# Split-ahead weight units moved from SyncE's DMA queue to GpSimd's, with four smaller edits of order

## The chip, the cores and the metric

One NeuronCore of one Trainium2 chip runs the whole program. The metric is device time in microseconds (us) of that core, from the first to the last instruction and what lies around them. The engines named below are PE (TensorE), DVE (VectorE), ACT (ScalarE), POOL (GpSimd) and SP (SyncE, which only issues DMAs here). Each engine runs its own instructions strictly in the program's order; a DMA queue's transfers are issued by the engine that owns it, in that engine's order.

## The reference

Two layers on a sequence of 512 rows of width 1024, all in f32. A layer is a SwiGLU feed-forward block (FFN), a mixer, and a second FFN:

```
for i in range(2):
    x = x + 0.5 * swiglu_ffn(x, ffn1_norm[i], gate[i], up[i], down[i])
    h = rmsnorm(x, mix_norm[i])
    x = x + (even_mixer(h, ...) if i == 0 else odd_mixer(h, ...))
    x = x + 0.5 * swiglu_ffn(x, ffn2_norm[i], ...)
return rmsnorm(x, final_norm)
# swiglu_ffn: h = rmsnorm(x, g); (silu(h @ w_gate) * (h @ w_up)) @ w_down, with d_ff = 2816
# even_mixer: gMLP and an attention with compressed, selected and window branches, then @ w_out
# odd_mixer: two sparse attentions, then @ w_out
```

## The kernel before

Every large product is made of three matmuls in a rounded f32 format: a weight is cut into a high part `h` (an ACT copy, line 315) and the rest `l` (a DVE subtraction, line 316), an activation likewise, and `mm3` (lines 320 to 322) adds h*h, h*l and l*h. A weight unit is a tile of 128 x 1024 numbers, 512 KB.

**FFN weights** are loaded by SP (lines 296, 309, 683), cut by ACT and DVE and used at once; the pools `raw`, `wh` and `wl` have four buffers each. An FFN has 11 strips `k` of 256 columns in three groups (0 to 3, 4 to 7, 8 to 10). For a strip `gate_up` multiplies x by the gate weights, ACT applies Silu (line 765), GpSimd multiplies by the norm's factor (line 766), and `seven` makes the up product in seven quarter products, whose results ACT and DVE take out of PSUM (`k1`, line 726, and others). After a group, `proj_T` multiplies by the down weights.

**Mixer weights** are cut ahead of time. `cut_ahead` is a generator over 60 units (32 of the even mixer, 28 of the odd one): it loads a unit (`craw`, two buffers), cuts it into `ch` and `cl` (two buffers each), and stores both to DRAM (`cuth`, `cutl`). The mixers later load the two parts and cut nothing. The generator is stepped by `take` after some strips and by `weave` inside the down products. What finally decides the order on each engine is a scheduler, which moves these units earlier than the code has them wherever it thinks an engine free; so most units of the odd mixer too are cut during the first FFN.

**The first chunks of x** are transposed by PE into PSUM (line 871); `Norm.add` copies each of the eight to `x[c]` (DVE, line 522), and makes the high part `h` (ACT, line 523) and the low part `l` (DVE, line 524) that the first matmuls read.

**Norms.** `Norm.rstd` sums squares with PE (line 549) and takes a power on GpSimd (line 553); `rstd_row` spreads the result over a bank (line 561); `finish` ends strip 0, which waited for it. **load_early** loads the compressor's weights on ACT's DMA queue. In the even mixer `branches` rotates the queries (`rope`, line 251, on DVE) and then transposes them (line 871) after two `yield`s; `weave` puts filler matmuls between yields.

Of the kernel before, what the change touches and what calls it, by code (L numbers as in the profile page):

```python
# [13 lines left out]
F32 = mybir.dt.float32  # L14
F32R = mybir.dt.float32r
I32 = mybir.dt.int32
AF = mybir.ActivationFunctionType
# [48 lines left out]
def hybrid_kernel(tc, x_in, positions, ffn1_norm, ffn1_w_gate, ffn1_w_up, ffn1_w_down, mix_norm,  # L66
# [4 lines left out]
    with ExitStack() as ctx:  # L71
# [199 lines left out]
        def cut_ahead(units):  # L271

            raw = None
            for i, (key, src, a, b, rows) in enumerate(units):
                n = a * b
                if raw is None:
                    raw = load_raw(src, a, b, rows, "craw", 2)
                h, l = cut(raw, n, ("ch", "cl"), 2)
                if i + 1 < len(units):
                    raw = load_raw(*units[i + 1][1:], "craw", 2)  # L280
                parts = []
                for t, c in ((h, "h"), (l, "l")):
                    d = scr.tile([P, n], F32, tag=nm("cut" + c), name=nm("cut" + c))
                    nc.sync.dma_start(d, t[:, :n].bitcast(F32))
                    parts.append(d)
                cut_units[key] = parts
                yield

        def load_raw(src, a, b, rows, tag, bufs):
            n = a * b  # L290
            raw = sb.tile([P, 1024], F32, tag=tag, bufs=bufs, name=nm(tag))
            r3 = raw[:, :n].rearrange("p (a b) -> p a b", a=a)
            if rows:
                o = 0
                for sap in src:
                    pin(nc.sync.dma_start(r3[:, o:o + sap.shape[1]], sap))
                    o += sap.shape[1]
            elif isinstance(src, list):
                o = 0
                for sap, wd in src:  # L300
                    dst = r3[:, :, o:o + wd]
                    if len(sap.shape) == 4:
                        for c in range(a):
                            nc.sync.dma_start(dst[:, c].rearrange("p (k d) -> p k d", k=sap.shape[2]), sap[:, c])
                    else:
                        nc.sync.dma_start(dst, sap)
                    o += wd
            else:
                nc.sync.dma_start(r3, src)
            return raw  # L310
# [188 lines left out]
        class Norm:  # L499
# [17 lines left out]
            def add(self, c, src=None):  # L517

                g = gcol(self.which, self.layer, c)
                h, l = tile_("xg"), tile_("xg")  # L520
                if src is not None:
                    pin(nc.vector.tensor_copy(x[c], src))
                pin(nc.scalar.activation(h, x[c] if src is None else src, AF.Copy, scale=g))
                pin(nc.vector.scalar_tensor_tensor(l, x[c], g, h.bitcast(F32), op0=ALU.mult, op1=ALU.subtract))
                self.xg[c] = (h, l)
# [216 lines left out]
        def gate_up(wg, wu, k, norm, sums, at):  # L742
# [6 lines left out]
            for hf in range(2):  # L749
                h, l = wunit(wg[hf * 512:(hf + 1) * 512, f0:f0 + 256].rearrange("(c p) f -> p c f", p=P), 4, 256)  # L750
                if hf:
                    norm.finish()
                for f in range(2):
                    if f:
                        norm.rstd()
                    for c in range(4):
# [17 lines left out]
        def ffn(norm, wg, wu, wd, nxt, hook=None, ahead=iter(()), per=2, early=None):  # L774

            sums = Sums(norm)
            for p0, p1 in GROUPS:
                at = []
                for k in range(p0, p1):
                    gate_up(wg, wu, k, norm, sums, at)  # L780
                    if hook is not None and k < 6:
                        next(hook, None)
                    if k in (3, 5, 6, 7, 8, 9):
                        run(take(ahead, 1))
                for d0 in range(0, D, 256):
                    part = per / (4 * (p1 - p0)) if p1 < 11 or d0 < 512 else 0.0
                    run(weave(proj_T(wd[256 * p0:256 * p1], at, d0,
                                     lambda c, ps: update(c, ps, 0.5, nxt if p1 == 11 else None)), ahead, [part]))
                    if p1 == 11 and d0 == 512 and early is not None:
                        early()  # L790
# [302 lines left out]
        def even_mixer(norm, nxt, tab):  # L1093
# [174 lines left out]
            def branches(g):  # L1268
# [7 lines left out]
                rope(zq[NT], 0, NT, 4, tab)  # L1276
                yield
                yield
                qrot = []
# [312 lines left out]
```

## Time and profile before

| | us |
|---|---|
| median of 3 runs | 2017.83 (2011.75 to 2018.38) |
| profiled execution | 2025.39 |
| its span, first to last instruction | 2023.3 |
| PE busy in the span | 1964.5 (97%) |
| DVE, ACT, POOL busy | 1394.1, 889.1, 306.4 |

The profiled execution is one run, 7.6 us above the median. The share of busy time is a mean over stages: the first FFN (0 to about 400 us) keeps the DMA engines at 70 to 94% and PE has gaps there, while from 750 to 1400 us PE has next to none. "PEclk" is the clock that was granted to TensorE, 1.00 being 2.4 GHz; its other level is 1.2 GHz.

### The profile page before, as it was taken

What the parts mean: (1) busy time and instruction counts of PE and PEld (TensorE: products, weight loads), DVE (VectorE), ACT (ScalarE), POOL (GpSimd) and SP (SyncE); (2) the same over time, 40 slices, a digit from 0 to 9 for tenths busy, and PEclk for the clock granted to TensorE, in tenths of its full rate; (3) what the DMA queues carried; (4) which work ended last, traced back from release to release, by engine and by line L of the source; (5) the groups of instructions that cost most, each with busy time, mean ns of one, the idle gap of its engine ahead of it and who ended that gap; (6) DMA issues with size and microseconds to landing.
All of it is one profiled execution on the core that took longest, in us unless ns stands there. A gap on an engine that the chain in (4) does not pass through costs nothing.

```text
span 2023.3 us, 30245 instructions
## 1 busy us (share of the span) xinstructions
PE 1964.5 (97%) x11575; PEld 1738.2 (86%) x11575; DVE 1394.1 (69%) x2456; ACT 889.1 (44%) x1562; POOL 306.4 (15%) x370
## 2 busy tenths in 40 slices
PE   8999998999999999999999999999999999999998
PEld 6888888799987889898888889888999788889898
DVE  6877758655587587475667747566698788567464
ACT  5544434424567564243345424333336764334143
POOL 1201101012234211010101101010112202011012
PEclk9999999999999999999999999999999999999999
DMA  7698899988210223333232333323532232323321
GB/s 223 209 305 268 296 303 313 335 299 294 105 43 26 89 85 111 98 95 115 84 105 84 116 93 101 109 84 100 191 143 105 73 102 85 116 84 105 104 84 63
DMA packets 223873, 290.35 MB, mean 144 GB/s; under 512 B 26136, under 2 KB 191728, under 8 KB 223728
## 3 DMA queue, kind: packets, MB, share of 16 engines
q1 hardware_dynamic: 216800, 282.01, 42.9%
q10 hardware_dynamic: 6736, 6.37, 0.9%
q8 instruction: 91, 1.49, 0.3%
q14 instruction: 54, 0.44, 0.1%
q0 software_dynamic: 192, 0.04, 0.0%
HBM read 230.11 MB, written 58.26 MB: 143 GB/s over the span
## 4 chain that ended last, share of the span: by engine, by line
PE 62%; DVE 8%; ACT 2%; issue 1%; POOL 0%; ACTq 0%; POOLq 0%; DVEq 0%
PE psB L320 8%; PE psB L321 8%; PE psB L322 8%; PE psT L322 6%; PE psT L320 6%; PE psT L321 6%; PE psG L320 5%; PE psG L322 5%; PE psG L321 5%; PE psC L949 2%; DVE f L1417 1%; PE psT L939 1%; DVE sm L1416 1%; DVE p L916 1%; ACT p L918 1%
## 5 line engine op out<-in xcount | busy, mean ns | idle before, releaser
L316 DVE TENSOR_TENSOR wl<-raw,wh 128x1024 fp32r<-128x1024 f32 (+1 forms) x198 | 259.9, 1315 | 82.5 <-ACT wh L315 77.8
L315 ACT ACTIVATE wh<-raw 128x1024 fp32r<-128x1024 f32 (+1 forms) x198 | 197.4, 1003 | 219.9 <-PE psB L321 181.5
L766 POOL TENSOR_TENSOR p<-p,p 128x512 f32<-128x512 f32 x78 | 127.9, 1641 | 992.9 <-ACT p L765 954.3
L320 PE MATMUL psT<-xg,wh 128*128 128x512 f32 x704 | 275.6, 392 | 0.2 <-DVE k L734 0.2
L322 PE MATMUL psT<-xg,wl 128*128 128x512 f32 x704 | 274.8, 391 | 0.0
L321 PE MATMUL psT<-xg,wh 128*128 128x512 f32 x704 | 274.8, 390 | 0.0
L321 PE MATMUL psB<-f,wh 128*128 128x512 f32 x656 | 255.6, 390 | 1.8 <-DVE f L495 1.8
L320 PE MATMUL psB<-f,wh 128*128 128x512 f32 x656 | 255.6, 390 | 0.0
L322 PE MATMUL psB<-f,wl 128*128 128x512 f32 x656 | 255.2, 389 | 0.0
L320 PE MATMUL psG<-t7h,wh 128*128 128x256 f32 x624 | 180.3, 289 | 12.2 <-ACT k L726 9.5
L322 PE MATMUL psG<-t7h,wl 128*128 128x256 f32 x624 | 179.0, 287 | 3.6 <-DVE wl L694 3.6
L321 PE MATMUL psG<-t7l,wh 128*128 128x256 f32 x624 | 178.9, 287 | 0.0
L322 PEld LDWEIGHTS psT<-xg,wl 128*128 128x128 f32 x704 | 132.7, 189 | 27.9
L320 PEld LDWEIGHTS psT<-xg,wh 128*128 128x128 f32 x704 | 132.8, 189 | 27.0 <-DVE k L734 0.4
L321 PEld LDWEIGHTS psT<-xg,wh 128*128 128x128 f32 x704 | 132.6, 188 | 26.5
L320 PE MATMUL psB<-wh,xg 128*128 128x256 f32 x512 | 148.2, 289 | 2.3 <-DVE sa L916 1.3
L321 PEld LDWEIGHTS psB<-f,wh 128*128 128x128 f32 x656 | 123.2, 188 | 27.7 <-DVE f L495 2.6
L322 PE MATMUL psB<-wh,xg 128*128 128x256 f32 x512 | 145.4, 284 | 0.0
L321 PE MATMUL psB<-wl,xg 128*128 128x256 f32 x512 | 145.3, 284 | 0.0
L765 ACT ACTIVATE p<-p 128x512 f32<-128x512 f32 x78 | 49.2, 631 | 218.3 <-DVE p L764 218.1
L322 PEld LDWEIGHTS psB<-f,wl 128*128 128x128 f32 x656 | 123.2, 188 | 25.5
L320 PEld LDWEIGHTS psB<-f,wh 128*128 128x128 f32 x656 | 123.2, 188 | 25.3
(304 smaller groups left out, 4661.3 us busy)
## 6 DMA issues: line engine op xcount, KB each, us to landing
raw<-in_ffn_w_down_dram SPq DMA_DIRECT2D x168, 256.0 KB, 3.4
raw<-in_ffn_w_gate_dram SPq DMA_DIRECT2D x80, 512.0 KB, 3.8
raw<-in_ffn_w_up_dram SPq DMA_DIRECT2D x80, 512.0 KB, 4.0
cuth<-ch SPq DMA_DIRECT2D x44, 512.0 KB, 6.6
cutl<-cl SPq DMA_DIRECT2D x44, 512.0 KB, 6.7
wh<-cuth SPq DMA_DIRECT2D x44, 512.0 KB, 4.4
wl<-cutl SPq DMA_DIRECT2D x44, 512.0 KB, 4.0
craw<-in_od_w_in_dram SPq DMA_DIRECT2D x16, 512.0 KB, 6.6
```

Source lines behind the costliest of these rows:

```text
L315: pin(nc.scalar.activation(h[:, :n], raw[:, :n], AF.Copy))
L316: pin(nc.vector.tensor_sub(l[:, :n], raw[:, :n], h[:, :n].bitcast(F32)))
L320: nc.tensor.matmul(ps, lh, rh, start=start, stop=False)
L321: nc.tensor.matmul(ps, lh, rl, start=False, stop=False)
L322: nc.tensor.matmul(ps, ll, rh, start=False, stop=stop)
L765: nc.scalar.activation(g, g, AF.Silu)
L766: nc.gpsimd.tensor_mul(g, g, rb)
L916: nc.vector.tensor_tensor_reduce(out=pr[i], in0=bank[i], in1=bias(i), scale=-1.0, scalar=3e38, op0=ALU.add, op1=ALU.min, accum_out=ng[:, i ...
L918: nc.scalar.activation(pr[i], pr[i], AF.Exp, scale=-1.0, bias=ng[:, i:i + 1], accum_out=rs[:, i:i + 1])
L939: nc.tensor.transpose(ps[:, o:o + P], pr[i][:, j * P:(j + 1) * P], ident)
L949: nc.tensor.matmul(job["accs"][0][:, j * P:512], v(j), hl[j][part], start=first, stop=last)
L1416: nc.vector.max(out=m8, in_=bd[i])
```

## The change

Five edits:

1. `cut_ahead` issues its loads and its stores from GpSimd's queue, and stores a unit one step later, after the next unit's cut. 214 DMAs leave SP's queue and enter POOL's.
2. `Norm.add` makes `h` and `l` of the first chunks straight from PSUM; the copy to `x[c]` comes after them, on ACT.
3. `gate_up` of strip 1 calls `rstd` 12 matmuls later, and `finish` likewise.
4. The generator is no longer stepped after strips 8 and 9, and `load_early` runs after the first quarter of the last down product, not after the third.
5. `branches` yields YB = 5 times, not twice, between the rotation and the transposes.

```diff
         def cut_ahead(units):
-            raw = None
+            raw = done = None
+
+            def store():
+                key, n, tiles = done
+                parts = []
+                for t, c in zip(tiles, "hl"):
+                    d = scr.tile([P, n], F32, tag=nm("cut" + c), name=nm("cut" + c))
+                    nc.gpsimd.dma_start(d, t[:, :n].bitcast(F32))
+                    parts.append(d)
+                cut_units[key] = parts
+
             for i, (key, src, a, b, rows) in enumerate(units):
                 n = a * b
                 if raw is None:
-                    raw = load_raw(src, a, b, rows, "craw", 2)
-                h, l = cut(raw, n, ("ch", "cl"), 2)
+                    raw = load_raw(src, a, b, rows, "craw", 2, nc.gpsimd)
+                now = key, n, cut(raw, n, ("ch", "cl"), 2)
+                if done is not None:
+                    store()
+                done = now
                 if i + 1 < len(units):
-                    raw = load_raw(*units[i + 1][1:], "craw", 2)
-                parts = []
-                for t, c in ((h, "h"), (l, "l")):
-                    d = scr.tile([P, n], F32, tag=nm("cut" + c), name=nm("cut" + c))
-                    nc.sync.dma_start(d, t[:, :n].bitcast(F32))
-                    parts.append(d)
-                cut_units[key] = parts
+                    raw = load_raw(*units[i + 1][1:], "craw", 2, nc.gpsimd)
                 yield
-
-        def load_raw(src, a, b, rows, tag, bufs):
+            store()
+
+        def load_raw(src, a, b, rows, tag, bufs, queue=nc.sync):
...
                 h, l = tile_("xg"), tile_("xg")
+                v = x[c] if src is None else src
+                pin(nc.scalar.activation(h, v, AF.Copy, scale=g))
+                pin(nc.vector.scalar_tensor_tensor(l, v, g, h.bitcast(F32), op0=ALU.mult, op1=ALU.subtract))
                 if src is not None:
-                    pin(nc.vector.tensor_copy(x[c], src))
-                pin(nc.scalar.activation(h, x[c] if src is None else src, AF.Copy, scale=g))
-                pin(nc.vector.scalar_tensor_tensor(l, x[c], g, h.bitcast(F32), op0=ALU.mult, op1=ALU.subtract))
+                    pin(nc.scalar.copy(x[c], src))
...
                 if hf:
-                    norm.finish()
+                    norm.rstd()
                 for f in range(2):
-                    if f:
-                        norm.rstd()
+                    if hf and f:
+                        norm.finish()
...
-                    if k in (3, 5, 6, 7, 8, 9):
+                    if k in (3, 5, 6, 7):
                         run(take(ahead, 1))
...
-                    if p1 == 11 and d0 == 512 and early is not None:
+                    if p1 == 11 and d0 == 0 and early is not None:
                         early()
...
-                yield
-                yield
+                for _ in range(YB):
+                    yield
```

Where the change adds lines ahead of them, later lines have higher numbers after it: 766 is 777, 871 is 882, 315 is 325.

On POOL, between the products of strips 2 to 4 of the first FFN (p is the Silu result, tile p_1541 is strip 4's), there was nothing else before:

```order
L766 TENSOR_TENSOR p_673<-p_673,p_427 128x512
L766 TENSOR_TENSOR p_677<-p_677,p_427 128x512
L766 TENSOR_TENSOR p_886<-p_886,p_427 128x512
L766 TENSOR_TENSOR p_890<-p_890,p_427 128x512
L766 TENSOR_TENSOR p_1541<-p_1541,p_427 128x512
L766 TENSOR_TENSOR p_1545<-p_1545,p_427 128x512
```

The same place now, from two DMAs ahead of strip 3's products on (craw is a load, cuth and cutl are stores):

```order
L282 DMA cuth_1893<-ch_1460 128x1024
L316 DMA craw_1897<-in_ev_w_in_dram 128x4x256
L777 TENSOR_TENSOR p_886<-p_886,p_427 128x512
L777 TENSOR_TENSOR p_890<-p_890,p_427 128x512
L282 DMA cutl_1895<-cl_1461 128x1024
L282 DMA cutl_2113<-cl_1890 128x1024
L282 DMA cuth_2111<-ch_1889 128x1024
L316 DMA craw_2115<-in_ev_w_in_dram 128x4x256
```

50 DMAs now stand between strip 3's second product and strip 4's first, and 44 between strip 7's and strip 8's.

On ACT, at the start of the program, the first rows before were these (xg is a chunk's high part, wh the first FFN weights', p_153 a square):

```order
L523 ACTIVATE xg_112<-psX_107,keep 128x512
L315 ACTIVATE wh_120<-raw_117 128x512
L531 ACTIVATE p_153<-x_92 128x512
L523 ACTIVATE xg_131<-psX_126,keep 128x512
L315 ACTIVATE wh_139<-raw_136 128x512
L315 ACTIVATE wh_170<-raw_167 128x1024
```

and they are these now:

```order
L532 ACTIVATE xg_112<-psX_107,keep 128x512
L325 ACTIVATE ch_1068<-craw_1065 128x840
L535 COPY x_92<-psX_107 128x512
L325 ACTIVATE wh_120<-raw_117 128x512
L532 ACTIVATE xg_131<-psX_126,keep 128x512
L542 ACTIVATE p_153<-x_92 128x512
L325 ACTIVATE ch_1102<-craw_1072 128x840
L535 COPY x_93<-psX_126 128x512
L325 ACTIVATE wh_139<-raw_136 128x512
```

The first split-ahead cuts (ch) have moved ahead of the first FFN weights' cuts. The second of the two DMAs that fill craw_1065 waits for the first.

On PE, in the even mixer, the transposes of the rotated queries (z_4200) of the first head group stood seven filler matmuls into a weight strip, eight together:

```order
L322 MATMUL psB_4462<-wh_4543,xg_3575 128x256
L320 MATMUL psB_4462<-wh_4543,xg_3588 128x256
L871 MATMUL psX_4523<-keep,z_4200 128x128
L871 MATMUL psX_4523<-keep,z_4200 128x128 x3
L871 MATMUL psX_4550<-keep,z_4200 128x128 x4
L321 MATMUL psB_4462<-wl_4545,xg_3588 128x256
```

They now stand 24 matmuls into it, in two fours with nine matmuls between:

```order
L332 MATMUL psB_4462<-wh_4532,xg_3698 128x256
L882 MATMUL psX_4574<-keep,z_4200 128x128
L882 MATMUL psX_4574<-keep,z_4200 128x128 x3
L330 MATMUL psB_4463<-wh_4532,xg_3616 128x256
L331 MATMUL psB_4463<-wl_4534,xg_3616 128x256
L332 MATMUL psB_4463<-wh_4532,xg_3617 128x256
```

## Rows read from the trace of the kernel before

**Rows 1.** The page: engines' busy time; GpSimd's product by the norm's factor.

```profile
PE 1964.5 (97%) x11575; PEld 1738.2 (86%) x11575; DVE 1394.1 (69%) x2456; ACT 889.1 (44%) x1562; POOL 306.4 (15%) x370
...
L766 POOL TENSOR_TENSOR p<-p,p 128x512 f32<-128x512 f32 x78 | 127.9, 1641 | 992.9 <-ACT p L765 954.3
```

**Rows 2.** Windows of the first 500 us, by stage.

```profile
core 0: us, PE busy (x) PEld busy (x) DVE busy (x) ACT busy (x) POOL busy (x), PEclk, DMA share, GB/s
0.00:44.00 44.00, 36.75 (x153) 28.47 (x153) 31.43 (x48) 24.77 (x34) 2.98 (x23) 0.96 0.72 220
44.00:103.00 59.00, 54.93 (x284) 47.59 (x285) 48.37 (x68) 31.53 (x42) 16.27 (x14) 0.97 0.71 217
103.00:309.00 206.00, 198.91 (x1073) 172.54 (x1072) 146.20 (x206) 83.21 (x108) 14.51 (x9) 0.99 0.88 291
309.00:356.00 47.00, 41.29 (x238) 36.97 (x237) 40.85 (x53) 26.16 (x35) 7.70 (x5) 0.93 0.94 322
356.00:460.00 104.00, 99.11 (x630) 91.40 (x630) 61.82 (x133) 37.44 (x68) 14.80 (x24) 0.98 0.90 316
460.00:500.00 40.00, 37.02 (x297) 36.55 (x296) 20.55 (x40) 19.73 (x39) 6.58 (x10) 0.96 0.87 299
```

**Rows 3.** Waits of PE, whole span: us in total, times, longest us.

```profile
PE psG L320 <- ACT k L726: 9.5, 5, 5.3
PE psX L871 <- DVE z L251: 6.4, 5, 3.0
...
PE psS L321 <- DMA wl<-cutl: 2.6, 1, 2.6
```

**Rows 4.** Waits of ACT, whole span: the longest of those for split-ahead DMAs.

```profile
ACT ch L315 <- DMA craw<-in_ev_w_in_dram: 23.9, 8, 5.6
```

**Rows 5.** DMA issues: engine, count, KB each, median us to landing.

```profile
cuth<-ch SPq DMA_DIRECT2D x44, 512.0 KB, 6.6
...
craw<-in_ev_w_in_dram SPq DMA_DIRECT2D x4, 384.0 KB, 5.0
...
craw<-in_ev_w_in_dram SPq DMA_DIRECT2D x4, 36.0 KB, 2.4
```

**Rows 6.** Timeline of ACT at strips 3, 4, 8, 9: start, duration, [idle before].

```profile
102.62 0.61 ACT L765 ACTIVATE p<-p 128x512 f32<-128x512 f32 x1
...
166.15 0.63 ACT L765 ACTIVATE p<-p 128x512 f32<-128x512 f32 x1 [3.52 <-DVE p L764]
...
308.56 1.06 ACT L315 ACTIVATE ch<-craw 128x1024 fp32r<-128x1024 f32 x1 [6.45 <-DMA craw<-in_od_w_in_dram]
309.53 0.61 ACT L765 ACTIVATE p<-p 128x512 f32<-128x512 f32 x1
...
336.46 0.62 ACT L765 ACTIVATE p<-p 128x512 f32<-128x512 f32 x1
```

**Rows 7.** Timeline of POOL: its DMAs (16, 16 and 4 rows).

```profile
67.61 0.78 POOL L63 DMA_DIRECT2D rows<-in_mix_norm_dram  x1
...
69.89 0.48 POOL L63 DMA_DIRECT2D rows<-in_ev_cmp_pos_v_dram  x1
70.36 0.52 POOL L63 DMA_DIRECT2D pos_i<-in_positions_dram  x1
```

**Rows 8.** Timeline of the opening, ACT then PE.

```profile
6.66 0.62 ACT L315 ACTIVATE wh<-raw 128x512 fp32r<-128x512 f32 x1
...
23.49 0.90 ACT L315 ACTIVATE ch<-craw 128x840 fp32r<-128x840 f32 x1 [3.01 <-DMA craw<-in_ev_w_in_dram]
...
25.54 0.49 PE L320 MATMUL psS<-xg,wh 128*128 128x512 f32 x1 [1.80 <-ACT xg L523]
```

**Rows 9.** Timeline of PE, even mixer and norm of the second FFN.

```profile
484.21 0.28 PE L322 MATMUL psB<-wh,xg 128*128 128x256 f32 x1
484.33 0.28 PE L320 MATMUL psB<-wh,xg 128*128 128x256 f32 x1
487.59 1.94 PE L871 MATMUL psX<-keep,z 128*128 128x128 f32 x8 [2.98 <-DVE z L251]
...
721.85 1.19 PE L549 MATMUL psX<-keep,p 128*128 128x2 f32 x8 [1.96 <-DVE p L535]
```

More of the change, by code (lines that the diff above doesn't have):

```diff
@@ L295, in load_raw @@
                 for sap in src:
-                    pin(nc.sync.dma_start(r3[:, o:o + sap.shape[1]], sap))
+                    pin(queue.dma_start(r3[:, o:o + sap.shape[1]], sap))
                     o += sap.shape[1]
@@ L303, in load_raw @@
                         for c in range(a):
-                            nc.sync.dma_start(dst[:, c].rearrange("p (k d) -> p k d", k=sap.shape[2]), sap[:, c])
+                            queue.dma_start(dst[:, c].rearrange("p (k d) -> p k d", k=sap.shape[2]), sap[:, c])
                     else:
-                        nc.sync.dma_start(dst, sap)
+                        queue.dma_start(dst, sap)
                     o += wd
             else:
-                nc.sync.dma_start(r3, src)
+                queue.dma_start(r3, src)
             return raw
```

## The prediction

> **What bounds the kernel now.** I read the page first: PE is busy 97% of the span, no other engine over 69% [rows 1]. So a gain can only come out of PE's idle time and out of the time in which its clock is low. The windows say where that is [rows 2]. For each stage the reader is to see two losses: length minus PE busy, and (1 - PEclk) times length, since a stretch at 1.2 GHz does half the work. They give 7.2 + 1.8 us for 0 to 44, 4.1 + 1.8 for 44 to 103, 7.1 + 2.1 for 103 to 309, 5.7 + 3.3 for 309 to 356, 4.9 + 2.1 for 356 to 460, and 3.0 + 1.6 for 460 to 500. So 44 to 356 us, the first FFN's strips and down products, loses 24.1 us, and all 500 us lose 45.
>
> Then the waits of PE [rows 3]: the longest is for `k1`, an ACT copy in `seven`, up to 5.3 us at once. ACT's timeline says why [rows 6]: at 308.56 it starts a split-ahead cut after waiting 6.45 us for that unit's load, and strip 8's Silu and the `k1` copy stand behind it in ACT's order. One group of such waits alone holds ACT 23.9 us in all [rows 4]. In the same stages the DMA engines are busy 71 to 94% [rows 2]. So PE is stalled here by an in-order ACT that waits for split-ahead data.
>
> **The change, part by part.** The 0.3% by which a measurement of this kernel can tell a change from none is 6 us.
>
> *A, the opening.* Removed: eight DVE copies; ACT's wait of 3.01 us for the second unit, which stood between two chunks and gave PE a gap of 1.80 us [rows 8], after which the clock lost the stage's 1.8 us [rows 2]. The second unit's cut has moved ahead of the second weights' cut and the third comes after seven weight cuts, so this should go: -3.6. Added: the first unit's cut stands ahead of the first weights' cut on ACT, and its second load waits for its first to land. With the load issued at about 1 us and the medians 5.0 and 2.4 us [rows 5], the cut can start at 8.4; with 2.4 for each, at about 5.8, when the chunk's own high part is just done. The cut takes 0.90, the copy of x about 0.6, and the weights' cut, which began at 6.66 [rows 8], begins between 7.5 and 9.9: 0.9 to 3.2 late, with PE waiting. I take 1.6, nearer the low end, because the loads now go out first. A = -2.
>
> *B, strips and down products to strip 9.* The units are not only on another queue, the scheduler also places them earlier. Counted in ACT's order, the cuts that stand ahead of strip 3's second Silu are 13 (8 before), of strip 8's first 55 (40 before), of strip 9's second 60 (43 before). ACT can't pass a cut before its load has landed and the store two units back has left its buffer, so these bytes must have moved by then. Between strip 3 (102.62) and strip 8 (309.53) [rows 6] there are now 42 units, 57.1 MB of loads and stores, beside 36 FFN weight units of 0.524 MB, 18.9 MB: 76.0 MB. Before it was 32 units and 60.3 MB, and 291 GB/s for 206 us, 59.9 MB, is what the windows have [rows 2]. How fast can it go? The two fullest stages moved 322 GB/s at a share of 0.94 and 316 at 0.90 [rows 2], 343 and 351 at a full share; I take 347. About 3.5 MB are in flight ahead of need at the start, as before. (76.0 - 3.5) / 0.347 = 209 us, so strip 8's Silu comes at 311.6 in place of 309.5. From there to strip 9's second Silu 9.9 MB take 28.5 us: 340.1 against 336.46 [rows 6]. PE's own work between strips 3 and 8 would need 207 less the 9.2 us lost there, 198, so DMA decides: B = +3, with the 24.1 us of old losses already inside it. Ends: if the queues leave the share at 0.94 (322 GB/s), 225 and 31 us give 358.5, B = +22; if DMA never binds, all the losses go, B = -24.
>
> By the Trainium skill's page DMA: Bandwidth & Descriptors, section Issuing engines are not separate DMA queues, DMAs started by different engines run on the same 16 DMA engines and interleave, and a second issuer saves only the time to issue. By that rule the move itself gains nothing in B (rival 3 below); the trace agrees so far that the shares are those of a nearly full resource, and no run here shows two full queues.
>
> What the second queue can do is keep the share up. SP's loads of FFN weights no longer stand behind stores that wait for a cut, and the split-ahead chain no longer behind weight loads that wait for a buffer. That is why I take the full share.
>
> POOL pays for it. Its DMAs with 4 to 16 rows cost 0.48 to 0.78 us each [rows 7], as much with 4 as with 16. A DMA of 128 rows costs 0.5 us if it goes by the instruction, 6.2 us if by the row (0.78 x 8). Between strip 3's product and strip 4's, 50 DMAs have to go out in about 62 us, 1.24 us each. I take 0.8, since 4 and 16 rows cost the same, and 50 x 0.8 = 40 fits into 62. The products themselves (1.64 us, [rows 1]) are needed only after `seven`, so a few us of lateness cost nothing. If this cover is gone, it is rival 2.
>
> *C, 356 to 460 us.* Before, the last cuts stood in the down product of strips 8 to 10 and in the even mixer; now none does. The wait of 2.6 us for the mixer's first weight unit [rows 3] came while DMA was 90% busy, and the clock lost 2.1 us in that stage [rows 2]. About 4.7 of the 7.0 us lost there go. With `load_early` moved into the emptier place: C = -5. It is between 0 (the loads still come late) and -7.
>
> *D, YB.* PE waited 2.98 us for the rotation [rows 9]. 17 more filler matmuls, 0.12 us apart [rows 9], now stand ahead: 2.0 us of the wait filled, and a gap of 1.0 should leave the clock alone (1.6 us lost in that stage, [rows 2]). D = -3.5, between 0 and -4.6; the later jobs start that much later, which PE's other filler covers.
>
> *E, rstd and finish.* In the second FFN PE waited 1.96 us before the sums of squares [rows 9]. In the built order these matmuls keep their place among the strip's matmuls, only the transposes of `rstd_row` move by 12. So the wait stays: E = 0 (to -3.7 if it went).
>
> Sum: -2 + 3 - 5 - 3.5 = -7.5 us. Against the profiled execution's 2025.4 that is 2017.9; that run lay 7.6 above the median of the runs shown, 2017.8, so for runs like those I expect **2010 us**.
>
> **The rivals.**
>
> 1. *The bytes bind harder (slower).* The split chain has two buffers at each step, and each step waits for a landing; stores took 6.6 us to land [rows 5]. If the share stays at 0.94, B is +22 and the sum +11.5: 2029. It decides the sign from B = +10.5, that is from 337 GB/s on downward (82.4 MB in 244.4 us). For it: no stage so far was over 0.94. Against it: in all of them weights and split units shared one queue.
>
> 2. *POOL becomes the bound (slower).* 214 DMAs and 22 products have to go through it by strip 10. At 1.5 us for a DMA that is 357 us, where there are about 334: B = +23 and the time 2030; at 2 us it would be over 2100. It decides from about 1.3 us per DMA. For it: nothing in the trace shows a POOL DMA of 128 rows. Against it: 4 rows cost as much as 16.
>    The Trainium skill's page SBUF: State Buffer, section SBUF: two separate sides, speaks for this rival: GpSimd writes the descriptors of its DMAs itself, and a DVE operation in a two-port mode locks it out meanwhile. Its figures, 620 ns for a DMA alone and about 3100 beside a DVE copy, would make 133 or 663 us of the 214, no change of the sum or a loss of hundreds. No run here shows it; DVE's work in this stage is mostly two-input subtractions, not copies.
>
> 3. *The queue doesn't matter.* ACT waits for the same bytes at the same places, its lead eaten by the earlier cuts: B = 0, A = 0, C half. With D that is -6 at best, -3 if the filled wait turns up at the next transposes: 2012 to 2015, which I count as the same.
>
> 4. *DMA never binds (faster).* With its own queue the chain runs ahead of ACT, and PE's 24 us go: sum -34.5, 1983. For it: the present waits come from late issues as well as from full engines. Against it: 76 MB in the 198 us that PE needs are 384 GB/s, more than any stage had.
>
> **How the numbers follow.** Chances: my forecast (2003 to 2017) 0.37, rival 1 0.17, rival 2 0.12, rival 3 0.17, rival 4 and what lies between it and the forecast 0.17. The forecast's range reaches six parts in seven below 2011.8, the bound of faster; counting a part of it and rival 3 as the same: faster 0.48, same 0.24, slower 0.28. The range, 1988 to 2036, leaves out the lower half of rival 4 and the upper part of rivals 1 and 2, about 2 in 10.
>
> **What would show it.** A: PE's first product matmuls 1 to 3 us later than now, and no gap before the fifth chunk. B: strip 8's first Silu at 305 to 318 us, the DMA share above 0.94 between 103 and 336, and ACT's waits for split-ahead loads longer, not shorter; POOL's DMAs at 0.5 to 1 us. C: no wait of PE for the mixer's first unit. D: the wait before the rotated transposes at 1 us or less. E: the wait before the sums still near 2 us. I am wrong if POOL's products start many us after their Silu, if the share stays where it is, or if strip 8 comes before 300 us.

## The result: 2083.6 us, 3.3% slower

The changed kernel takes 2083.62 us (median of 4 runs, 2079.16 to 2087.26) where the kernel before takes 2016.91 (4 runs beside it): a ratio of 1.0334 [1.0305, 1.0364]. The forecast was 2010, the range ended at 2036. The profiled execution of the changed kernel took 2085.85 us, its span 2084.1; against the 2023.3 us of before, 60.8 us more.

The page of the changed kernel: busy time of the engines, and the two DMA queues (packets, MB, share of the 16 engines' time). [rows 1] has the same line of before.

```profile
PE 1979.7 (95%) x11575; PEld 1751.5 (84%) x11575; DVE 1389.0 (67%) x2448; ACT 893.2 (43%) x1570; POOL 430.2 (21%) x584
...
q1 hardware_dynamic: 161152, 197.75, 29.6%
q0 software_dynamic: 23776, 84.30, 11.6%
```

GpSimd's queue (q0) now carries 84.30 MB. POOL has 214 instructions more and is busy for 123.8 us more; one of these DMAs lasts 0.64 us on the mean (a store 0.55, a load 0.73 to 0.76). No engine but PE is near its limit.

Its windows, cut where the same strips begin and end as in [rows 2] (52, 111, 364 and 419 us answer to 44, 103, 309 and 356):

```profile
0.00:52.00 52.00, 37.55 (x164) 29.45 (x165) 33.82 (x47) 33.46 (x48) 20.37 (x48) 0.99 0.91 297
52.00:111.00 59.00, 53.64 (x274) 46.28 (x273) 47.54 (x65) 31.60 (x42) 31.16 (x43) 0.95 0.80 259
111.00:364.00 253.00, 210.67 (x1061) 182.01 (x1060) 160.95 (x214) 94.11 (x118) 101.44 (x151) 0.90 0.89 306
364.00:419.00 55.00, 45.90 (x245) 41.20 (x245) 40.55 (x53) 23.42 (x32) 19.33 (x24) 0.87 0.59 210
419.00:522.00 103.00, 101.99 (x674) 95.48 (x674) 51.15 (x126) 29.22 (x63) 12.14 (x23) 1.00 0.56 193
```

Read as the prediction read them: the third row loses 42.3 us to idle time of PE and 25.3 to its clock, where before lost 7.1 and 2.1. The DMA share there is 0.89, as before (0.88): the second queue has not filled the engines. After 419 us PE is better off than before (1.0 us idle in 103, clock 1.00).

ACT's timeline: the Silu of strip 3 (the second), 4 (first), 8 (first) and 9 (second); [rows 6] has them of before at 102.62, 166.15, 309.53 and 336.46.

```profile
110.74 0.63 ACT L776 ACTIVATE p<-p 128x512 f32<-128x512 f32 x1 [0.21 <-DVE p L775]
...
193.80 0.63 ACT L776 ACTIVATE p<-p 128x512 f32<-128x512 f32 x1 [2.17 <-DVE p L775]
...
364.41 0.63 ACT L776 ACTIVATE p<-p 128x512 f32<-128x512 f32 x1 [5.75 <-DVE p L775]
...
396.95 0.61 ACT L776 ACTIVATE p<-p 128x512 f32<-128x512 f32 x1
```

They are 8.1, 27.7, 54.9 and 60.5 us late. So the opening and strips 0 to 3 lost 8.1 us, the stretch from there to strip 9 52.4, and all that follows 0.3. Where the largest single step lies, between 160 and 191 us, ACT's timeline shows how (ch is a split-ahead cut; wh at L325 and L704 is an FFN weight's):

```profile
160.99 1.06 ACT L325 ACTIVATE ch<-craw 128x1024 fp32r<-128x1024 f32 x1 [4.53 <-DMA craw<-in_ev_w_out_dram]
161.95 1.04 ACT L325 ACTIVATE wh<-raw 128x1024 fp32r<-128x1024 f32 x1
170.71 0.63 ACT L325 ACTIVATE ch<-craw 128x512 fp32r<-128x512 f32 x1 [7.71 <-DMA craw<-in_ev_w_out_dram]
171.25 0.61 ACT L704 ACTIVATE wh<-raw 128x512 fp32r<-128x512 f32 x1
177.24 1.06 ACT L325 ACTIVATE ch<-craw 128x1024 fp32r<-128x1024 f32 x1 [5.38 <-DMA craw<-in_ev_w_out_dram]
178.20 1.04 ACT L704 ACTIVATE wh<-raw 128x1024 fp32r<-128x1024 f32 x1
181.22 0.63 ACT L325 ACTIVATE ch<-craw 128x512 fp32r<-128x512 f32 x1 [1.97 <-DMA cuth<-ch]
186.77 1.06 ACT L325 ACTIVATE ch<-craw 128x1024 fp32r<-128x1024 f32 x1 [4.92 <-DMA craw<-in_ev_w_out_dram]
187.73 1.04 ACT L704 ACTIVATE wh<-s 128x1024 fp32r<-128x1024 f32 x1
```

Each weight's cut stands right behind a split-ahead cut that waits 4.5 to 7.7 us for its load. DVE makes the low parts of the same weights (wl), and it waits for other data: for the landing of a split-ahead store that must leave its buffer, and for the up weights of the FFN, which it adds to sums (s).

```profile
179.51 1.22 DVE L326 TENSOR_TENSOR cl<-craw,ch 128x1024 fp32r<-128x1024 f32 x1 [5.73 <-DMA cutl<-cl]
...
181.25 1.21 DVE L705 TENSOR_TENSOR wl<-raw,wh 128x1024 fp32r<-128x1024 f32 x1
...
190.21 0.69 DVE L720 TENSOR_TENSOR s<-raw,raw 128x512 f32<-128x512 f32 x1 [7.14 <-DMA raw<-in_ffn_w_up_dram]
...
191.95 1.22 DVE L705 TENSOR_TENSOR wl<-s,wh 128x1024 fp32r<-128x1024 f32 x1
```

The waits of PE between 170 and 194 us (in total, times, longest):

```profile
PE psG L330 <- ACT wh L704: 6.4, 2, 3.8
PE psG L332 <- DVE wl L705: 6.3, 2, 3.6
```

PE waits 12.7 us for just these cuts, half of it for ACT's and half for DVE's, in gaps of 2.6 to 3.8 us, and the clock falls to its lower level for part of the time. The window has:

```profile
170.00:194.00 24.00, 11.25 (x51) 9.37 (x52) 9.24 (x12) 6.61 (x9) 9.43 (x16) 0.72 0.84 286
```

PE is busy for 11.25 of 24 us, at a mean clock of 0.72.

### The profile page after: what moved, and what is told of

It reads as the page before. It is cut to its first block, busy times and chain, and to the rows that moved or that the text cites. A ratio compares the mean times of both kernels' runs of the same rounds, so it can differ in the third digit from the quotient of the medians.

```text
span 2084.1 us, 30295 instructions
## 1 busy us (share of the span) xinstructions
PE 1979.7 (95%) x11575; PEld 1751.5 (84%) x11575; DVE 1389.0 (67%) x2448; ACT 893.2 (43%) x1570; POOL 430.2 (21%) x584
## 3 DMA queue, kind: packets, MB, share of 16 engines
q0 software_dynamic: 23776, 84.30, 11.6%
## 4 chain that ended last, share of the span: by engine, by line
PE 61%; issue 12%; DVE 12%; DMA 9%; POOL 3%; ACT 3%; DVEq 0%; POOLq 0%; ACTq 0%
PE psB L330 8%; PE psB L331 8%; PE psB L332 8%; PE psT L331 5%; PE psT L330 5%; PE psT L332 5%; PE psG L330 5%; PE psG L332 5%; PE psG L331 5%; DMA cutl<-cl 4%; DMA raw<-in_ffn_w_up_dram 2%; DMA craw<-in_ev_w_in_dram 2%; DVE cl L326 1%; ACT p L929 1%; DVE f L1428 1%
## 5 line engine op out<-in xcount | busy, mean ns | idle before, releaser
L777 POOL TENSOR_TENSOR p<-p,p 128x512 f32<-128x512 f32 x78 | 123.2, 1582 | 758.2 <-ACT p L776 730.4
L325 ACT ACTIVATE wh<-raw 128x1024 fp32r<-128x1024 f32 (+1 forms) x198 | 197.4, 1003 | 189.8 <-PE psB L331 162.1
L330 PE MATMUL psG<-t7h,wh 128*128 128x256 f32 x624 | 185.1, 297 | 25.0 <-ACT k L737 22.1
L332 PE MATMUL psG<-t7h,wl 128*128 128x256 f32 x624 | 183.8, 294 | 6.7 <-DVE wl L705 6.7
L330 PEld LDWEIGHTS psG<-t7h,wh 128*128 128x128 f32 x624 | 127.1, 204 | 27.9 <-ACT k L737 23.6
L332 PE MATMUL psG<-xg,wl 128*128 128x256 f32 x468 | 135.1, 289 | 15.9 <-DVE wl L705 15.9
```

What stands on the lines that cost most here:

```text
L325: pin(nc.scalar.activation(h[:, :n], raw[:, :n], AF.Copy))
L330: nc.tensor.matmul(ps, lh, rh, start=start, stop=False)
L332: nc.tensor.matmul(ps, ll, rh, start=False, stop=stop)
L777: nc.gpsimd.tensor_mul(g, g, rb)
```

## The experiments

The question is first whether the queue, the earlier place of the cuts or the other edits cost the time (theories Q, P and O), then what of a second queue costs it: that the queues share the DMA engines (S), GpSimd's own issuing (G), or stores that block loads (B). All ratios are to the kernel before.

| run | us | ratio [95%] |
|---|---|---|
| changed kernel | 2083.62 | 1.0334 [1.0305, 1.0364] |
| e1 all but the queue | 2015.81 | 0.9995 [0.9982, 1.0007] |
| e2 GpSimd's queue, cuts held back | 2071.69 | 1.0269 [1.0247, 1.0291] |
| e3 odd units behind the first FFN | 2097.19 | 1.0391 [1.0366, 1.0417] |
| e4, e17 copies on ScalarE alone | 2007.76, 2011.78 | 0.9955 [0.9937, 0.9973], 0.9977 [0.9967, 0.9987] |
| e5 as e2, ScalarE's queue | 2046.20 | 1.0148 [1.0131, 1.0165] |
| e6 as e2, loads alone on GpSimd's | 2079.59 | 1.0310 [1.0287, 1.0334] |
| e7, e18 as e4, odd units in program order | 2004.05, 2004.50 | 0.9937 [0.9922, 0.9951], 0.9940 [0.9923, 0.9957] |
| e8 as e4, YB | 2013.62 | 0.9982 [0.9973, 0.9992] |
| e9 as e2, a quarter of the bytes | 2027.88 | 1.0056 [1.0041, 1.0071] |
| e10 as e1, a quarter of the bytes | 2012.23 | 0.9976 [0.9964, 0.9988] |
| e11 changed kernel, a quarter of the bytes | 2046.97 | 1.0152 [1.0134, 1.0171] |
| e12 changed kernel, odd units in program order | 2047.51 | 1.0148 [1.0131, 1.0165] |
| e13 as e6, ScalarE's queue | 2058.31 | 1.0198 [1.0161, 1.0236] |
| e14 as e2, odd units in program order | 2045.11 | 1.0138 [1.0107, 1.0169] |
| e15 changed kernel, copies on VectorE | 2068.44 | 1.0253 [1.0222, 1.0284] |
| e16 as e4, edits 3 and 4 | 2013.28 | 0.9987 [0.9973, 1.0000] |

**Queue, place or the rest: e1 to e4.** e1 takes `cut_ahead` and `load_raw` of before, in everything else the changed kernel:

```diff
-                    raw = load_raw(*units[i + 1][1:], "craw", 2, nc.gpsimd)
+                    raw = load_raw(*units[i + 1][1:], "craw", 2)
...
-                    nc.gpsimd.dma_start(d, t[:, :n].bitcast(F32))
+                    nc.sync.dma_start(d, t[:, :n].bitcast(F32))
```

> The changed kernel with the split-ahead units back on SyncE's queue and stored in the same step; all the other edits stay. In ScalarE's order 42 cuts then stand ahead of strip 8's first Silu, where the changed kernel has 55 and the kernel before 40. Theory P (the cuts are placed earlier in ScalarE's and VectorE's in-order queues than their data can come): near the kernel before or a little under it, 2005 to 2020 us, because the placement is nearly that of before. Theory Q (the GpSimd queue itself is slower, wherever the cuts stand): 2005 to 2020 too. Theory O (the copies of x on ScalarE and the other edits cost the time): 2060 or more.

e2 keeps GpSimd's queue and ties each cut to a place behind a Silu, so that the 60 cuts stand in ScalarE's order against the Silus as they do in e1:

```diff
+        BEHIND = [4, 5, 6, 6, 6, 6, 9, 10, 17, 18, 20, 21, 23, 24, 29, 29, 42, 42, 44, 45, 48, 49]
...
+            if tags[0] == "ch":
+                behind = sum(b <= n_cut[0] for b in BEHIND) - 1
+                n_cut[0] += 1
+                if behind >= 0:
+                    tc.add_manual_dep(c.ins, silus[behind].ins.name, mybir.DependencyInfo(
+                        mybir.DependencyClass.NoSync, mybir.DependencyReason.DATA), reason="behind")
```

> The changed kernel with all units still on GpSimd's queue, but each split-ahead cut held behind the Silu behind which it stands when the units are on SyncE's queue (42 cuts ahead of strip 8's first Silu in place of 55; 17 ahead of strip 4's in place of 26). Theory P: the loss goes with the placement, within 10 us of the run with everything but the queue, 2005 to 2025. Theory Q: the loss stays, 2070 to 2090. Theory O: 2060 or more.

e3 is the changed kernel with `behind = 21 if n_cut[0] >= 32 else -1`.

> The changed kernel, but the 28 units of the odd mixer are held behind the last Silu of the first FFN; the 32 of the even mixer stand where the change put them. Theory P: up to strip 4, where the placement is that of the changed kernel (26 cuts), its 28 us of lateness stay; after strip 5 there are no cuts left in the way and the further 34 us go: 2045 to 2060. Theory Q: the units still go through GpSimd's queue and are only moved, so the loss is nearly all there or moves to where they now stand: 2065 to 2090.

e4 is the kernel before with edit 2 alone.

> The kernel before with one edit alone: ScalarE makes the copies of the first chunks of x in place of VectorE. Theories P and Q: within 10 us of the kernel before, 2010 to 2025. Theory O: 2040 or more. My prediction had -2 us for this edit together with the moved cuts.

e1 is back at the time before: edit 1, the queue together with the store one step later, costs all 67.8 us. e2 gives back 11.9 of them. So the earlier place (P), on which I would have staked the loss when I saw the trace, is the smaller part, and Q holds. e3 shows that place matters locally: without cuts behind strip 5 the lateness at strip 10's last Silu is 16.5 us against 62.8. But the 28 units, now crowded into the even mixer, cost 55 us there instead, and the run ends above both forecasts. e4 is faster than before by itself, so O falls.

**What of the queue: e5, e6, e13.** e5 and e6 are e2 with another queue:

```diff
-                    raw = load_raw(*units[i + 1][1:], "craw", 2, nc.gpsimd)
+                    raw = load_raw(*units[i + 1][1:], "craw", 2, nc.scalar)      # e5, e13
...
-                    nc.gpsimd.dma_start(d, t[:, :n].bitcast(F32))
+                    nc.scalar.dma_start(d, t[:, :n].bitcast(F32))                # e5
+                    nc.sync.dma_start(d, t[:, :n].bitcast(F32))                  # e6, e13
```

> The run with the cuts held back, but the split-ahead units go through ScalarE's hardware queue in place of GpSimd's (35 cuts ahead of strip 8's first Silu, fewer than in any run so far). What is asked is what of a second queue costs the 55 us that the held run lost. Theory S (two queues share the DMA engines, so the FFN's weights lose their place ahead of the split-ahead units; the up weights landed 7.1 us after their issue in the held run, 5.5 with one queue): the loss stays with a second hardware queue, 2050 to 2085, and the up weights land at 6.5 us or more. Theory G (it is GpSimd's own way of issuing, in order behind its products and waits, 0.5 to 0.8 us each): near the kernel before, 2005 to 2030, though ScalarE spends some 0.05 to 0.4 us on each issue. Theory P is not asked here: its share was 12 us.

> Held as before, but only the loads of split-ahead units go through GpSimd's queue; the stores are back on SyncE's. In the held run GpSimd waited 58 us for ScalarE's cuts before it could send off a store, with the next load behind it. Theory B (a store that waits for its cut blocks the next load in GpSimd's queue): most of the 55 us go, 2010 to 2035. Theory S: the read half of the second queue's traffic stays, a third of the bytes, so 2030 to 2060. Theory G: half of the DMAs stay on GpSimd: about 2040.

> The run with the loads alone on GpSimd's queue and the stores on SyncE's (2079.6 us), with ScalarE's hardware queue in GpSimd's place; the 60 cuts stand at the same places. Theory S (any second queue that carries the split-ahead loads beside the weights costs, as does SyncE blocked by stores that wait for cuts): 2060 to 2085. Theory G (the software queue of GpSimd: 0.75 us for an issue and loads that land 1.1 to 1.4 us later than on SyncE's): 2015 to 2035.

e6 speaks against B: with the stores off GpSimd's queue nothing is won, and the run is above all three forecasts. It is no clean test, because SyncE, which also issues the FFN's weights, now waits for the cuts. e5 and e13 fit neither S nor G alone. In e5 the up weights land at 5.7 us (median), less than S asked for, and from strip 3's second Silu (3.2 us late) to strip 10's (3.4) nothing is lost; its 30 us come from the opening and the even mixer. But ScalarE's own work holds these DMAs back: when a weight load goes out, 0.6 MB of split-ahead transfers are under way on the other queue, in e2 1.4 MB (means of 92 and 90 loads between 20 and 420 us, each transfer under way counted whole). With ScalarE's hardware queue the loads alone cost 42.5 us over e1, with GpSimd's 63.8, with the same cuts at the same places against the Silus. Some 5 us of e13 are its own: its first matmul starts at 8.22 us, since the norm's rows come behind split-ahead loads on ScalarE's queue. So a second queue costs whoever owns it, and GpSimd's costs 21 us more.

One rival was not tested alone. Every run with a second queue also stores a unit one step later, and e1 does not. The traces speak against it as the common cause: between 0 and 420 us ACT and DVE wait 33 us for the landing of split-ahead stores in e1, and only 14 in e6 and 8 in e13, which store late too. In the changed kernel these waits grow to 76 us, so there the stores have a share in the loss (DVE's wait at 179.51 above is one of them); how large it is was not measured.

**Bytes or issuing: e9 to e11.** The DMAs, waits and cuts stay, most split-ahead transfers move a quarter, and the mixers compute with repeated quarters of their weights:

```diff
-                    d = scr.tile([P, n], F32, tag=nm("cut" + c), name=nm("cut" + c))
-                    nc.gpsimd.dma_start(d, t[:, :n].bitcast(F32))
+                    d = scr.tile([P, n // 4], F32, tag=nm("cut" + c), name=nm("cut" + c))
+                    nc.gpsimd.dma_start(d, t[:, :n // 4].bitcast(F32))
...
+                    k = 1 if tag == "craw" else sap.shape[1]
+                    pin(queue.dma_start(r3[:, o:o + k], sap[:, :k]))
```

> The held run (2071.7 us, all units on GpSimd's queue) with the same number of DMAs, waits and cuts, but most of them move a quarter of the bytes: one chunk of each load and a quarter of the columns of each store, which the cuts and the later reads repeat, so the weights of both mixers are not the reference's. Theory S (the split-ahead bytes of a second queue take the DMA engines from the FFN's weights, whose up loads then land 7.1 us after their issue in place of 5.5): the loss goes, 1995 to 2015, and the up weights land at 5 us or less. Theory G (the loss is in GpSimd's issuing, its order and its waits, whatever the bytes): 2050 to 2072.

> All edits but the queue (2015.8 us), with the bytes of the split-ahead units cut to a quarter in the same way; the cuts stand where the scheduler puts them, all 60 ahead of strip 8's first Silu. This is the control for the next run. With little traffic both theories give 1995 to 2010.

> The changed kernel (2083.6 us) with the bytes of the split-ahead units cut to a quarter in the same way, and the cuts where the scheduler puts them (all 60 ahead of strip 8's first Silu, nearly as in the run before this one), on GpSimd's queue. Theory S: within 8 us of the run before this one. Theory G: 40 us or more above it.

e9 gives back 43.8 of e2's us: at that placement it is the bytes for the most part, though e9 stays 13 us above the range that S gave. (On SyncE's queue the quarter bytes are worth 3.6 us, e10 against e1, with denser cuts.) It is not that the DMA engines are full. Between strip 3's second Silu and strip 8's first the same 32 units are cut in e1 (98.0 to 302.4 us) and in e2 (108.5 to 334.3):

```profile
98.00:302.40 204.40, 196.58 (x1053) 170.18 (x1051) 147.83 (x206) 84.68 (x110) 14.65 (x9) 0.99 0.90 299
```

```profile
108.50:334.30 225.80, 200.26 (x1032) 172.04 (x1033) 147.75 (x207) 83.12 (x107) 84.37 (x123) 0.95 0.80 272
```

e2 takes 21.4 us longer while the engines' share falls from 0.90 to 0.80. DMA issues between 20 and 420 us show what happens to the FFN's up weights (count, KB each, median us to landing): e1, then e2, the changed kernel and e9.

```profile
raw<-in_ffn_w_up_dram SPq DMA_DIRECT2D x19, 512.0 KB, 5.6
```

```profile
raw<-in_ffn_w_up_dram SPq DMA_DIRECT2D x20, 512.0 KB, 7.1
```

```profile
raw<-in_ffn_w_up_dram SPq DMA_DIRECT2D x20, 512.0 KB, 9.1
```

```profile
raw<-in_ffn_w_up_dram SPq DMA_DIRECT2D x19, 512.0 KB, 4.3
```

Same queue, same transfer: it lands 1.5 and 3.5 us later when the split-ahead units are on GpSimd's queue. What DVE then waits for these weights between 0 and 420 us (in total, times, longest), e1 and e2:

```profile
DVE s L710 <- DMA raw<-in_ffn_w_up_dram: 8.7, 4, 3.8
```

```profile
DVE s L728 <- DMA raw<-in_ffn_w_up_dram: 39.7, 8, 7.4
```

This wait is the sign that all runs with a second queue and full bytes share: 24 to 40 us, against 9 to 13 in the runs with one queue. The landing time alone does not explain it: in e6, e13 and e14, which lose 64, 43 and 41 us, the median is 5.9, 5.7 and 5.3 us, near e1's 5.6. So there the up weights must go out later against the sums that need them, and why was not traced. One such delay in e2, engine by engine, SP (two loads in one row), POOL, DVE, ACT and PE:

```profile
188.14 4.45 SPq L702 DMA_DIRECT2D raw<-in_ffn_w_up_dram  x2
```

```profile
188.55 0.72 POOL L308 DMA_DIRECT2D craw<-in_ev_w_out_dram  x1
```

```profile
199.59 0.69 DVE L728 TENSOR_TENSOR s<-raw,raw 128x512 f32<-128x512 f32 x1 [5.69 <-DMA raw<-in_ffn_w_up_dram]
200.19 0.69 DVE L783 TENSOR_TENSOR p<-psT,p 128x512 f32<-128x512 f32 x1
```

```profile
200.91 0.63 ACT L784 ACTIVATE p<-p 128x512 f32<-128x512 f32 x1 [8.28 <-DVE p L783]
```

```profile
206.99 0.58 PE L338 MATMUL psG<-t7h,wh 128*128 128x256 f32 x1 [5.68 <-ACT k L745]
```

The up weights go out beside three of POOL's transfers. DVE waits 5.69 us for them with strip 5's first product behind it, ACT gets its Silu 8.28 us after it ran dry, the `k` copies come behind that and the second Silu, and PE stands for 5.68 us. The product needs none of the late weights; it is only queued behind them.

By the Trainium skill's page DMA: Bandwidth & Descriptors, section SWDGE vs HWDGE vs iDMA, each DMA engine takes turns between the queues that hardware and GpSimd feed. The landing times of e2 and the changed kernel agree with that, those of e6, e13 and e14 hardly show it.

e11 adds a second cause. Its cuts stand as densely as e10's (60 ahead of strip 8), few bytes move, and still it is 34.7 us over e10, so S's forecast of 8 is missed. Between strip 3's second Silu and strip 4's first it takes 80.6 us, e10 68.8. ACT's timeline of e11 there:

```profile
167.39 0.62 ACT L711 ACTIVATE wh<-raw 128x512 fp32r<-128x512 f32 x1
170.42 0.63 ACT L332 ACTIVATE ch<-craw 128x512 fp32r<-128x512 f32 x1 [2.42 <-DMA craw<-in_ev_w_out_dram]
173.15 0.69 ACT L332 ACTIVATE ch<-craw 128x584 fp32r<-128x584 f32 x1 [2.09 <-DMA craw<-in_od_w_in_dram]
174.64 0.69 ACT L332 ACTIVATE ch<-craw 128x584 fp32r<-128x584 f32 x1 [0.80 <-DMA craw<-in_od_w_in_dram]
175.24 1.04 ACT L711 ACTIVATE wh<-raw 128x1024 fp32r<-128x1024 f32 x1
```

Three cuts, each waiting for its own load, stand between two weight cuts and hold the second back. Its raw buffer comes free that much later; the up weights that go into it leave at 177.90 and land at 182.59, and PE's gap before the cut of their sums is 6.4 us. With two `craw` buffers a cut's load leaves when the cut two before it is done. On GpSimd's queue that took 1.7 us (mean of the 23 units cut between 110 and 200 us), on SyncE's 0.8 (24 units in e10), and the flight 3.9 and 3.7. An estimate from these: about 1 us for two units, over 21 units, is some 10 of the 12 us. The rest of the 34.7 us was not traced.

**Fewer units: e7, e12, e14, e18.** Each odd unit is held behind the Silu that was traced last when it was traced itself (`behind = len(silus) - 1` from unit 32 on), which puts them in the second and third FFN; e7 and e18 do it on SyncE's queue with edit 2, e12 in the changed kernel, e14 in e2.

> The kernel before with the copies of x on ScalarE (2007.8 us) and one more edit: each of the odd mixer's 28 split-ahead cuts is held behind the Silu that was traced last when the unit was traced, so they lie in the second and third FFN, where the DMA engines are a quarter busy, and none lies in the first FFN. Theory P (bytes and cuts in the first 420 us make PE wait): the losses behind strip 5 go, 10 to 20 us, 1988 to 1998. Rival (ScalarE's waits for split-ahead data there are covered by PE's lead, or the waits come back in the later stages): 2003 to 2010.

> The changed kernel, with the 28 units of the odd mixer in program order, in the second and third FFN, and none in the first. Where they were all held behind the last strip of the first FFN, the changed kernel's lateness fell to 16 us by that strip, and 55 us came back in the even mixer. Theory S (only where the DMA engines are nearly full does the second queue cost): in the emptier FFNs the 28 units cost at most 5 us, 2025 to 2040 in all. Theory G (each unit through GpSimd costs wherever it stands): 2050 to 2080.

> The held run on GpSimd's queue (2071.7 us) without the odd mixer's 28 units in the first FFN: they lie in program order in the second and third. On SyncE's queue the same move gave 2004 us. If the loss goes with the units that share the first 420 us with the FFN's weights: half of the units, 2025 to 2040. If each unit through GpSimd costs wherever it stands: 2050 to 2072. If half of the bytes already leave room enough: 2010 to 2020.

> The same with the odd mixer's units in program order, again: 2001 to 2007, 3 to 4 us below the run before it if the first result was no accident.

e12 lies between S's forecast and G's: 36 us under the changed kernel, yet 43 over e18. e14 is 40.6 us over e18, with the same cuts at the same places among the first FFN's Silus: half of the units in that FFN, yet three quarters of e2's loss. The loss does not go with their number; I had forecast 2025 to 2040. The Silus tell where it lies. Up to strip 7's last Silu the same 29 cuts stand ahead in e1, e2, e14 and e18, and there e2 is already 22 us behind e1 and e14 25 behind e18. Between there and the first rotated transposes of the even mixer e2 loses 30 us more, e14 only 4; it loses the other 16 behind them. A part of e14's 40.6 us belongs to edits 3 to 5, which e18 lacks (e1 is 4.0 us over e17). On SyncE's queue the same step is the fastest kernel of all, 12 us under the kernel before and 79 under the changed one. Against its own base it gains less than the 10 to 20 us forecast: 3.7 us (e7 against e4) and 7.3 (e18 against e17). Its windows between strip 3 and strip 8 of before, and the 47 us after (e18):

```profile
103.00:309.00 206.00, 202.02 (x1082) 175.05 (x1082) 146.77 (x210) 80.14 (x103) 15.91 (x10) 0.99 0.73 241
309.00:356.00 47.00, 47.00 (x288) 42.33 (x287) 33.01 (x45) 18.41 (x26) 7.37 (x5) 1.00 0.35 111
```

Against [rows 2] the DMA share is down from 0.88 and 0.94, and PE's idle time from 7.1 and 5.7 us to 4.0 and none.

**The other edits: e8, e15, e16, e17.** e8 is e4 with `for _ in range(YB)`; e16 is e4 with edits 3 and 4; e15 is the changed kernel with `Norm.add` of before; e17 is e4 again.

> The kernel before with the copies of x on ScalarE (2007.8 us) and one more edit: five steps of filler ahead of the rotated transposes in place of two. The run with every edit but the queue was 8 us slower than that with the copies alone, and lost it between 350 and 750 us. My prediction had -3.5 us for this edit: 2004. Rival (the filler ahead of the rotated transposes delays the jobs behind them): 2012 to 2018. If it comes out at 2006 to 2010 the edit is worth nothing and the 8 us belong to the split of the weights ahead of the mixer or to the earlier compressor loads.

> The kernel before with the copies of x on ScalarE, the split-ahead units left out of strips 8 and 9, the compressor weights sooner and the new order of rstd and finish: all edits but the queue and the filler step. My prediction's terms C and E together: 5 us below the run with the copies alone, 2003. From the run with all but the queue (2015.8) less that with copies and filler step (2013.6): 2 us above it, 2010. If C holds only with the units out of the way on a second queue: no difference, 2006 to 2010.

> The kernel before with ScalarE's copies alone, again, as the base for its two neighbours: 2005 to 2011.

> The changed kernel (2083.6 us) with the copies of x back on VectorE; 52 cuts then stand ahead of strip 8's first Silu in place of 55. On SyncE's queue the edit was worth -8.5 us. If it is worth the same beside GpSimd's queue: 2092. If the opening of the changed kernel is lost to the first split-ahead unit, for which ScalarE waits ahead of the first weights' cut, whoever copies: 2075 to 2088.

Neither e8 nor e16 is under its base: 1.8 and 1.5 us over e17, e8 5.9 over e4. e15 is 15 us faster than the changed kernel and under both of its forecasts: the edit that gains 5 to 9 us on one queue loses 15 beside GpSimd's. Strip 3's second Silu is as late in e15 (+9.5 us) as in the changed kernel, so it isn't lost in the opening. 52 cuts in place of 55 stand ahead of strip 8, and 22 in place of 26 ahead of strip 4; that this is the reason was only argued.

## Why the prediction was wrong

- **What bounds the kernel** was read rightly: an in-order ACT that waits for split-ahead data. It is the same chain now, with longer waits.
- **A** (-2 forecast, +8.1 measured) failed in its flight times. The chain is the one described: the first unit's cut ahead of the first weights' cut, its second load behind the landing of its first. I put that load at 2.4 to 5.0 us each. Beside the first weights and x the two took 6.2 and 5.9 (and PE's wait for the last chunks of x grew from 1.20 to 3.65 us). POOL's timeline of the changed kernel, then ACT's:

```profile
1.43 0.97 POOL L316 DMA_DIRECT2D craw<-in_ev_w_in_dram  x1 [0.36 <-issue]
...
7.93 0.72 POOL L316 DMA_DIRECT2D craw<-in_ev_w_in_dram  x1 [4.42 <-DMA craw<-in_ev_w_in_dram]
```

```profile
13.94 0.90 ACT L325 ACTIVATE ch<-craw 128x840 fp32r<-128x840 f32 x1 [7.87 <-DMA craw<-in_ev_w_in_dram]
14.75 0.57 ACT L535 COPY x<-psX 128x512 f32<-128x512 f32 x1
15.22 0.63 ACT L325 ACTIVATE wh<-raw 128x512 fp32r<-128x512 f32 x1
```

  The weights' cut starts at 15.22, 8.6 us after the 6.66 of [rows 8], not 0.9 to 3.2.
- **B** (+3 forecast, -24 to +22 the ends, +52.4 measured) failed at "what the second queue can do is keep the share up". It stayed at 0.89. The kernel moved the 76 MB in 253.7 us, 300 GB/s, and the break-even was 337. I took the rate from the two fullest stages, while the stage itself had 291 GB/s [rows 2]; with 291 my own sum gives B = +49, close to what was measured. But a sum of bytes would not have been the reason: e2 moves the same units as e1 and loses 21.4 us between strips 3 and 8 with the engines less busy. I treated the stretch as a question of capacity, bytes over a rate, and what e2 shows is engines that wait, in order, for landings. I had asked what ACT's cuts would wait for, and never what the weights' loads would, which I counted as freed by the move; in the changed kernel they landed 3.5 us later, and DVE waited 32.9 us for the up weights where it had waited 9.9.
- **POOL's price** (0.8 us, measured 0.64) was near, and **rival 2** as priced falls: POOL is no bound. The 3100 ns beside a DVE copy that the Trainium skill gives (page SBUF — State Buffer, section SBUF: two separate sides) are shown by no run here; the longest issue on POOL was 0.97 us.
- **C, D and E** (-8.5 together, +0.3 measured from strip 9 on). The waits that I wanted gone are gone: after strip 9 PE no longer waits for the mixer's first unit or before the rotated transposes. Nothing came of it. In e4, without edits 4 and 5, PE's waits for the rotation between 340 and 600 us are 0.8 us in all, so D filled a wait that edit 2's new order closes by itself; e8 and e16 give no gain. E was right, the wait before the sums is still 2.0 us.
- **The rivals.** Rival 1 named the mechanism that came, a share that stays and a two-buffer chain that waits for landings, with a chance of 0.17, and priced it at 2029. Rival 3, "the queue doesn't matter", was priced as a small gain; the runs show that the queue matters by more than any other edit.

What stays open: how the 21 us between GpSimd's and ScalarE's queue divide (an issue on POOL takes 0.2 to 0.3 us longer than one on ACT), why the up weights come too late in e6, e13 and e14 though they land nearly as fast as in e1, and what the later store costs by itself. Of the 67.8 us, 11.9 went with the place of the cuts, 43.8 with the bytes and 12.1 are left at quarter bytes; but e9 and e11 differ by 19.1, so place and queue are not independent, and this is one order of taking them away, not a unique division.

## What to carry to other kernels

The order of issue on a single queue is also a priority (e1's up weights land in 5.6 us with all units on their queue, e2's in 7.1), so before background traffic gets a queue of its own, ask how much later the foreground loads will land and what stands behind their readers in order. Where background work has hundreds of microseconds of slack, move it in time (e18, 7.3 us under e17), not to another queue. In a stage whose engines wait in order for landings, bytes over a rate are only the floor; ask also what each reader will wait for.

## What the runs showed of the hardware

- Two queues kept the DMA engines no busier than one: share 0.89 against 0.88 in the stage between strips 3 and 8 (306 and 291 GB/s).
- A 512 KB load of up weights on SyncE's queue landed after 9.1 us (median) beside GpSimd's transfers in the changed kernel, 7.1 in e2, and 5.6 in e1 and the kernel before.
- With a second queue, GpSimd's or ScalarE's, and full bytes, DVE waited 24 to 40 us for these weights in the first 420 us, with one queue 9 to 13.
- A GpSimd DMA of 128 rows took POOL 0.64 us on the mean of 214, one of 4 or 16 rows 0.48 to 0.78 [rows 7].
